# A head's eight output transposes: two at a time between the splits, or all in a row

## The chip, the cores and the metric

The kernel runs on one core of one Trainium2 chip. The metric is the device time of one execution in microseconds; the lower, the better.

## The reference

A decoder trunk of two layers on one sequence of 256 tokens and 2048 channels, in float32. Layer 0 mixes tokens by multi-scale retention with 8 heads (keys of 256, values of 512), layer 1 by a short gated convolution; each layer ends with a SwiGLU of width 5632. What matters here is the end of the retention:

```python
o = rms_norm(chunked_gated_linear_attention(q, k, v, log_a))   # per head: 256 tokens x 512
o = merge_heads(o).astype(h.dtype)
return ((jax.nn.silu(g) * o) @ w_out).astype(h.dtype)
```

For each head, the output is normed per token, multiplied by its gate, and the 8 heads side by side (256 tokens x 4096) are multiplied by `w_out`. All inputs and the result are float32.

## The kernel before

**Numbers in two parts.** Matrix products run in a reduced form of float32 (`F32R`). Each number is therefore kept as a `hi` part (a cast) and a `lo` part (the number less its `hi`), and a product is three partial products: hi by hi, hi by lo, lo by hi. Weights come from memory in pieces of 128 x 2048 (`raw`, three buffers); `prepare` makes of each half a `hi` (ScalarE, L312) and a `lo` (VectorE, L315), 128 x 1024, in a ring of four buffers each. `take` hands TensorE the next 128 columns and keeps two halves prepared ahead (`AHEAD`). The same is done to activations by `split` (L412): a cast on ScalarE (L414) and a subtraction on VectorE (L415), which reads the same source and the result of the cast.

**The layout.** Activations stand turned: channels on the 128 partitions, tokens along the free dimension, so a product gives turned outputs as well. The retention is the exception. `values` gives `v` with tokens on the partitions (`by_token`, L372 to L374), and so does `outputs` (L869) the head's result: two tiles `o` of 128 tokens x 512 channels. Before `w_out` these have to be turned: 2 tiles x 4 blocks of 128 x 128, eight transposes on TensorE (a product with the identity `ident`).

**The order of a head.** `projections` (L915) makes q and k (`packed`, L397 to L399, then `rope`), `values`, `scores`, and the gates `sg`. `mixed` (L856) returns three pieces of work that are put off into the next head: `outputs(0)`, `last_outputs`, `ends`. `ticked` (L340) counts TensorE's steps and runs a piece when `STEPS` = (8, 8, 20) steps have gone by since the one before. So `ends` stands 20 steps behind the outputs, amid the next head's projections; for the fourth and the last head of `HEAD_ORDER` it stands amid the first group of `ret_out`, the product with half of `w_out` (L357, L360). Between `last_outputs` and `ends`, the norm is made: a sum of squares on ScalarE (L872), a root (`roots_of`, L445 on VectorE, L447 on GpSimd), and `o` (L878 on VectorE).

**`ends`.** It goes through the four blocks of 128 channels. Two blocks share a PSUM bank of 128 x 512: block 0 and 1 the first bank, 2 and 3 the second. For each block it turns both `o` tiles into its half of the bank, then splits that half into `mid[n]`, the operand of `ret_out`.

**What sets the order.** TensorE's instructions run in the order of the program text. Those of ScalarE and VectorE are ordered in this stage by a scheduler from a model of their durations. Each engine then works through its list in order and waits on semaphores. There are eight PSUM banks, one tag, given out by `bank()` (L335). The framework puts waits between engines that use one bank, also where they use different halves of it. The modulation vectors are made on the side through the whole kernel: `modulation` (L241) fetches a row block and reduces it on VectorE (L246).

Of the kernel before, what the change touches and what calls it, by code (L numbers as in the profile page):

```python
# [17 lines left out]
P = 128  # L18
# [169 lines left out]
def trunk(ctx: ExitStack, tc: tile.TileContext, x_in, c_in, pos_in, w_mod, cols_in, tab_in, w_all, out):  # L188
    nc = tc.nc
# [7 lines left out]
    def name(s):  # L197
        serial[0] += 1
        return f"{s}_{serial[0]}"

    def tmp(tag, shape=(P, S), dtype=F32, pool=work, bufs=None):
        return pool.tile(list(shape), dtype, tag=tag, name=name(tag), bufs=bufs)
# [24 lines left out]
    inv_freq, ident = tab[:, 0:1], tab[:, 1 : 1 + P]  # L227
# [107 lines left out]
    def bank():  # L335
        return ps.tile([P, 2, S], F32, tag="bank", name=name("bank"))
# [75 lines left out]
    def split(dst, src, at=slice(0, S)):  # L412

        nc.scalar.copy(dst[:, 0, at], src)  # L414
        nc.vector.tensor_tensor(dst[:, 1, at], src, dst[:, 0, at].bitcast(F32), op=ALU.subtract)  # L415
# [12 lines left out]
    def norm_sums(accs):  # L428

        pt = bank()  # L430
        for t in range(2):
            for i, acc in enumerate(accs):
                nc.tensor.matmul(
                    pt[:, 0, t : t + 1], acc[:, t * P : (t + 1) * P], ones[:, 0:1],
                    start=i == 0, stop=i == len(accs) - 1,
                )
        return pt
# [4 lines left out]
    def roots_of(total, n):  # L442

        r = tmp("rs", (P, 2), bufs=4)
        nc.vector.tensor_scalar(r, total, 1.0 / n, EPS, op0=ALU.mult, op1=ALU.add)  # L445
        r2 = tmp("rs", (P, 2), bufs=4)
        nc.gpsimd.tensor_tensor(r2, r, half, op=ALU.pow)  # L447
        return r2
# [117 lines left out]
    with ExitStack() as inner:  # L566
# [52 lines left out]
        def rm_tile(key, dtype=F32):  # L619
            tag_of[key] = free.pop(0)  # L620
            return rm.tile([P, 2, S], dtype, tag=tag_of[key], name=name("rm"))
# [9 lines left out]
        with tc.tile_pool(name="start", bufs=1) as sp:  # L631
# [59 lines left out]
            with tc.manual_schedule(engines={mybir.EngineType.DVE, mybir.EngineType.Activation}):  # L691
# [16 lines left out]
                for i in range(0, D, 2 * S):  # L708
                    pt = bank().rearrange("p a b -> p (a b)")
# [24 lines left out]
                pt = norm_sums([acc[0][:, 0, :]])  # L734
# [65 lines left out]
        mid = [None] * (4 * HEADS)  # L800
# [55 lines left out]
        def mixed(head, both, v, sg):  # L856

            total = tmp("osum", (P, 2), bufs=2)
            pts, os = [], []

            def outputs(t):

                pt = bank().rearrange("p a b -> p (a b)")
                pts.append(pt)
                n = 0
                for jt in range(t + 1):
                    sp = both[jt][:, :, (t - jt) * P : (t - jt + 1) * P]
                    for i, j in ((0, 0), (0, 1), (1, 0)):
                        nc.tensor.matmul(pt, sp[:, i, :], v[:, jt, j, :], start=n == 0, stop=n == 3 * t + 2)  # L869
                        n += 1  # L870
                sq = rp.tile([P, DV], F32, tag="o", name=name("sq"), bufs=2)
                nc.scalar.activation(sq, pt, AF.Square, accum_out=total[:, t : t + 1])  # L872

            def normed_outputs():
                r = roots_of(total, DV)
                for t, pt in enumerate(pts):
                    o = rp.tile([P, DV], F32, tag="o", name=name("o"), bufs=2)
                    nc.vector.scalar_tensor_tensor(o, pt, r[:, t : t + 1], sg[t], op0=ALU.mult, op1=ALU.mult)  # L878
                    os.append(o)

            def last_outputs():
                outputs(1)
                normed_outputs()

            def ends():
                for i in range(4):
                    if i % 2 == 0:
                        pt = bank()
                    for t, o in enumerate(os):
                        nc.tensor.transpose(  # L890
                            pt[:, i % 2, t * P : (t + 1) * P], o[:, i * P : (i + 1) * P], ident
                        )
                    n = 4 * head + i
                    mid[n] = rm_tile(("mid", n), F32R)
                    split(mid[n], pt[:, i % 2, :])

            return list(zip(STEPS, [lambda: outputs(0), last_outputs, ends]))

# [70 lines left out]
    mid = [mpool.tile([P, 2, S], F32R, tag=f"mid{i}", name=name("mid")) for i in range(KT)]  # L969
# [81 lines left out]
```

## Time and profile before

| | |
|---|---|
| median of three runs | 2684.3 us (2682.71 to 2688.37) |
| the profiled execution | 2684.12 us, its span 2682.3 us |
| mean granted clock of TensorE | 0.992 |
| TensorE busy, share of the span | 98% |
| VectorE, ScalarE busy | 74%, 47% |
| memory read | 682.99 MB, 255 GB/s over the span |

The span goes from the first to the last instruction. An engine's busy time is the union of its instructions. TensorE's matmuls are pipelined: the record of one ends after the next could begin, so intervals between starts tell more than lengths. PE is the matmuls, PEld the weight loads in front of them, DVE is VectorE, ACT ScalarE, POOL GpSimd. A row of the timeline gives start, length, engine, line, operation, what is written and read, a count of instructions merged into the row, and in brackets the idle time before it with the instruction that ended it. A row of the waits gives total, number and longest. A row of the windows gives the stretch, then busy time and count for each engine, the granted clock of TensorE (1.00 is full), the share of the transfers and their GB/s.

### The profile page before, as it was taken

The numbers are of one execution on the slowest core, as the hardware profiler recorded it, in microseconds if no ns is written. First come the engines' busy times: TensorE is split into PE (matmuls) and PEld (weight loads), VectorE is DVE, ScalarE is ACT, GpSimd is POOL, SyncE is SP. The second block draws the span as 40 slices with busy tenths as digits, with TensorE's granted clock in tenths as the row PEclk, the third lists the DMA queues.
The fourth block names the chain that finished last, engine by engine and source line by source line (L and its number), as shares of the span: only waits on it lengthen the run. The fifth ranks groups of instructions, "written<-read, shape, count | busy, mean of one in ns | idle before, by whom it ended". The sixth has DMA issues, their size and how long they took to land.

```text
span 2682.3 us, 38239 instructions
## 1 busy us (share of the span) xinstructions
PE 2627.3 (98%) x15220; PEld 2303.8 (86%) x15220; DVE 1993.6 (74%) x2543; ACT 1248.4 (47%) x1770; POOL 145.8 (5%) x230
## 2 busy tenths in 40 slices
PE   7999899999999999999999999999999999999998
PEld 6988789878889888888888898888998888888887
DVE  7997768777678887777777879888886765555564
ACT  5644443444446454334444454444554443444443
POOL 0000000100000001100000001100000000000000
PEclk9999999999999999999999999999999999999999
DMA  9966558866767887777777768776767665555553
GB/s 398 388 269 242 222 192 313 295 226 253 250 223 254 301 307 282 272 279 282 282 273 276 276 221 313 297 281 247 280 252 266 256 230 188 189 189 189 189 189 126
DMA packets 96950, 687.58 MB, mean 256 GB/s; under 512 B 10753, under 2 KB 12545, under 8 KB 13825
## 3 DMA queue, kind: packets, MB, share of 16 engines
q1 hardware_dynamic: 96770, 685.13, 68.8%
q8 instruction: 119, 1.95, 0.3%
q14 instruction: 61, 0.50, 0.0%
HBM read 682.99 MB, written 2.10 MB: 255 GB/s over the span
## 4 chain that ended last, share of the span: by engine, by line
PE 73%; issue 19%; DVE 4%; DMA 2%; ACT 1%; POOL 0%; DVEq 0%; ACTq 0%; POOLq 0%
PE bank L357 34%; PE bank L360 17%; PE bank L372 4%; PE bank L373 4%; PE bank L374 4%; PE bank L399 2%; PE bank L397 2%; PE bank L398 2%; PE bank L517 1%; PE bank L516 1%; PE bank L518 1%; DVE lo L315 1%; DMA raw<-w_all 1%; DVE raw L642 1%; DMA raw<-w_mod 1%
## 5 line engine op out<-in xcount | busy, mean ns | idle before, releaser
L315 DVE TENSOR_TENSOR lo<-raw,hi 128x1024 fp32r<-128x1024 f32 x912 | 1113.5, 1224 | 583.2 <-ACT hi L312 581.1
L312 ACT CAST hi<-raw 128x1024 fp32r<-128x1024 f32 x912 | 955.1, 1052 | 1118.4 <-PE bank L357 644.3
L357 PE MATMUL bank<-h,hi 128*128 128x512 f32 x3296 | 1155.3, 395 | 0.0
L360 PE MATMUL bank<-h,lo 128*128 128x256 f32 x3296 | 924.4, 280 | 0.0
L357 PEld LDWEIGHTS bank<-h,hi 128*128 128x128 f32 x3296 | 622.5, 189 | 145.3
L360 PEld LDWEIGHTS bank<-h,lo 128*128 128x128 f32 x3296 | 622.0, 189 | 0.0
L357 PE MATMUL bank<-mid,hi 128*128 128x512 f32 x1604 | 556.3, 393 | 0.0
L360 PE MATMUL bank<-mid,lo 128*128 128x256 f32 x1604 | 444.9, 277 | 0.1
L246 DVE SCALAR_TENSOR_TENSOR raw<-raw,cb 128x2048 f32<-128x2048 f32 x160 | 365.8, 2286 | 13.7 <-DMA raw<-w_mod 13.5
L357 PEld LDWEIGHTS bank<-mid,hi 128*128 128x128 f32 x1604 | 300.7, 187 | 69.4
L360 PEld LDWEIGHTS bank<-mid,lo 128*128 128x128 f32 x1604 | 301.3, 188 | 0.5 <-DVE lo L315 0.5
L372 PE MATMUL bank<-hi,h 128*128 128x512 f32 x512 | 206.1, 403 | 0.0
L373 PE MATMUL bank<-lo,h 128*128 128x512 f32 x512 | 205.3, 401 | 0.0
L374 PE MATMUL bank<-hi,h 128*128 128x512 f32 x512 | 205.0, 400 | 0.0
L357 PE MATMUL bank<-rm,hi 128*128 128x512 f32 x496 | 177.2, 401 | 0.0
L399 PE MATMUL bank<-h,lo 128*128 128x256 f32 x512 | 147.1, 287 | 6.8 <-DVE lo L315 6.8
L397 PE MATMUL bank<-h,hi 128*128 128x256 f32 x512 | 146.9, 287 | 2.5 <-ACT h L670 2.5
L398 PE MATMUL bank<-h,hi 128*128 128x256 f32 x512 | 146.5, 286 | 0.5 <-DVE h L671 0.5
L360 PE MATMUL bank<-rm,lo 128*128 128x256 f32 x496 | 139.9, 282 | 0.0
L374 PEld LDWEIGHTS bank<-hi,h 128*128 128x128 f32 x512 | 98.4, 192 | 23.4
L372 PEld LDWEIGHTS bank<-hi,h 128*128 128x128 f32 x512 | 98.7, 193 | 20.2
L373 PEld LDWEIGHTS bank<-lo,h 128*128 128x128 f32 x512 | 98.3, 192 | 20.1
(152 smaller groups left out, 2255.3 us busy)
## 6 DMA issues: line engine op xcount, KB each, us to landing
raw<-w_all SPq DMA_DIRECT2D x456, 1024.0 KB, 4.9
raw<-w_mod SPq DMA_DIRECT2D x192, 1024.0 KB, 5.0
x<-x_in SPq DMA_DIRECT2D x4, 512.0 KB, 5.6
out<-out SPq DMA_DIRECT2D x5, 256.0 KB, 2.9
decay<-tab_in SPq DMA_DIRECT2D x8, 128.0 KB, 2.1
out<-out SPq DMA_DIRECT2D x3, 128.0 KB, 2.3
out<-out SPq DMA_DIRECT2D x1, 384.0 KB, 2.7
cols<-cols_in SPq DMA_DIRECT2D x1, 160.0 KB, 8.7
```

The lines of the kernel that those rows point to most:

```text
L246: nc.vector.scalar_tensor_tensor(raw, raw, 1.0, cb, op0=ALU.mult, op1=ALU.mult, accum_out=total)
L312: nc.scalar.copy(hi, raw)
L315: nc.vector.tensor_tensor(lo, raw, hi.bitcast(F32), op=ALU.subtract)
L357: nc.tensor.matmul(pt, hi, h, start=fresh and k == g.ks[0], stop=False, skip_group_check=True)
L360: nc.tensor.matmul(pt[:, 1, :], lo, h[:, 0, :], start=False, stop=last and k == g.ks[-1], skip_group_check=True)
L372: nc.tensor.matmul(o, ht[:, 0, :], hi, start=first, stop=False)
L373: nc.tensor.matmul(o, ht[:, 0, :], lo, start=False, stop=False)
L374: nc.tensor.matmul(o, ht[:, 1, :], hi, start=False, stop=last)
L397: nc.tensor.matmul(pt, hi, h[:, 0, :], start=first, stop=False, skip_group_check=True)
L398: nc.tensor.matmul(pt, hi, h[:, 1, :], start=False, stop=False, skip_group_check=True)
L399: nc.tensor.matmul(pt, lo, h[:, 0, :], start=False, stop=last, skip_group_check=True)
L516: nc.tensor.matmul(pt, hi, rows[0], start=k == 0, stop=False)
```

## The change

The eight transposes are given first, tile by tile instead of block by block, into two banks that are taken at the start; the four splits follow.

```diff
             def ends():
+                turned = [bank() for _ in range(2)]
+                for t, o in enumerate(os):
+                    for i in range(4):
+                        nc.tensor.transpose(
+                            turned[i // 2][:, i % 2, t * P : (t + 1) * P], o[:, i * P : (i + 1) * P], ident
+                        )
                 for i in range(4):
-                    if i % 2 == 0:
-                        pt = bank()
-                    for t, o in enumerate(os):
-                        nc.tensor.transpose(
-                            pt[:, i % 2, t * P : (t + 1) * P], o[:, i * P : (i + 1) * P], ident
-                        )
                     n = 4 * head + i
                     mid[n] = rm_tile(("mid", n), F32R)
-                    split(mid[n], pt[:, i % 2, :])
+                    split(mid[n], turned[i // 2][:, i % 2, :])
```

Everything else is the same. In the built program the scheduler puts a head's four splits into the order of blocks 0, 2, 1, 3, with some pieces of other work between them, where before it was 0, 1, 2, 3. The transposes stand at L889 of the changed kernel (L890 before).

## The prediction

> **What bounds the kernel now.** I read the page first: the busy times, then the chain that ended last.
>
> ```profile
> span 2682.3 us, 38239 instructions
> PE 2627.3 (98%) x15220; PEld 2303.8 (86%) x15220; DVE 1993.6 (74%) x2543; ACT 1248.4 (47%) x1770; POOL 145.8 (5%) x230
> PE 73%; issue 19%; DVE 4%; DMA 2%; ACT 1%; POOL 0%; DVEq 0%; ACTq 0%; POOLq 0%
> ```
>
> TensorE (PE) is busy for 98% of the span and holds 73% of the chain. So a microsecond in which PE stands still is a microsecond of the result, if nothing else is late in its place. The change touches only the eight calls of `ends`, one per head, between 230 and 753 us. The next view is therefore the waits of PE and of its weight loads (PEld) from 225 to 780 us; the two answers have one row each (total us, times, longest).
>
> ```profile
> PE bank L890 <- DVE rm L415: 26.3, 16, 2.5
> PEld bank L890 <- DVE rm L415: 30.0, 16, 2.7
> ```
>
> In that half millisecond PE waits for nothing except this: a transpose (L890) waits for the second half of the split before it (L415 on VectorE), 16 times, twice per head. No row says that PE waits for a `lo` piece, a bank or a transfer. The timeline of the first head (start, length, engine, line, the idle before in brackets) shows why.
>
> ```profile
> 230.27 0.38 PE L890 MATMUL bank<-tab,o 128*128 128x128 f32 x2
> 230.28 1.22 DVE L315 TENSOR_TENSOR lo<-raw,hi 128x1024 fp32r<-128x1024 f32 x1
> 230.93 0.37 ACT L414 CAST rm<-bank 128x256 fp32r<-128x256 f32 x1
> ...
> 232.02 0.42 DVE L415 TENSOR_TENSOR rm<-bank,rm 128x256 fp32r<-128x256 f32 x1
> 232.50 0.42 PEld L890 LDWEIGHTS bank<-tab,o 128*128 128x128 f32 x4 [2.08 <-DVE rm L415]
> 232.50 0.66 PE L890 MATMUL bank<-tab,o 128*128 128x128 f32 x4 [1.85 <-DVE rm L415]
> ...
> 234.29 0.29 PEld L890 LDWEIGHTS bank<-tab,o 128*128 128x128 f32 x2 [1.38 <-DVE rm L415]
> ...
> 234.64 0.78 PE L372 MATMUL bank<-hi,h 128*128 128x512 f32 x1
> ```
>
> Two transposes go into the left half of a bank, ScalarE and VectorE split it, and only then do the next two go into the right half of the same bank. VectorE is still busy with a `lo` piece (230.28) and what stands behind it, so its part comes late, at 232.02. Note the run of four in 0.66 us: it is the right half of the first bank and the left half of the second, and it crosses from bank to bank without a wait. Only the return to a bank that is being read costs.
>
> The stall has a second price. I asked for busy time in stretches of 3.4 us (PE, PEld, DVE, ACT, POOL, then the granted clock), first a pair from the start of the span, which has no transposes, then two that hold stalls:
>
> ```profile
> 152.10:155.50 3.40, 1.48 (x12) 1.45 (x12) 3.40 (x6) 3.18 (x5) 0.00 (x0) 1.00 0.10 39
> 155.50:158.90 3.40, 3.40 (x12) 2.85 (x12) 3.40 (x4) 1.04 (x2) 0.00 (x0) 0.50 0.94 386
> 271.60:275.00 3.40, 1.78 (x10) 1.23 (x8) 3.40 (x4) 1.43 (x2) 0.19 (x1) 1.00 0.76 251
> 377.40:380.80 3.40, 1.59 (x10) 1.26 (x11) 1.53 (x5) 1.02 (x3) 0.00 (x0) 1.00 0.58 178
> ```
>
> then the stretches behind the stalls, of which the first, the last and the sum of all eight:
>
> ```profile
> 234.04:237.45 3.41, 3.15 (x9) 2.57 (x10) 0.63 (x2) 0.37 (x1) 0.00 (x0) 0.50 0.82 271
> ...
> 752.86:756.27 3.41, 3.41 (x13) 2.82 (x12) 1.68 (x2) 0.10 (x1) 0.00 (x0) 0.50 0.40 166
> sum 27.28, PE 26.16 PEld 22.55 DVE 15.47 ACT 4.77 POOL 0.69; mean PE 3.27 PEld 2.82 DVE 1.93 ACT 0.60 POOL 0.09
> ```
>
> After each of the eight stalls the granted clock is 0.50 for 3.41 us. A stretch in which PE was busy 1.59 us or less is followed by such a drop, also without a transpose (152.10 and 155.50); the one with 1.78 us (271.60) is not. What half the clock costs is seen from starts of neighbouring matmuls, wide ones around the second head:
>
> ```profile
> 272.54 0.39 PE L373 MATMUL bank<-lo,h 128*128 128x512 f32 x1
> 272.77 0.39 PE L374 MATMUL bank<-hi,h 128*128 128x512 f32 x1
> ...
> 280.38 0.63 PE L373 MATMUL bank<-lo,h 128*128 128x512 f32 x1
> 280.81 0.63 PE L374 MATMUL bank<-hi,h 128*128 128x512 f32 x1
> ```
>
> and narrow ones around the seventh:
>
> ```profile
> 667.44 0.28 PE L398 MATMUL bank<-h,hi 128*128 128x256 f32 x1
> 667.56 0.28 PE L399 MATMUL bank<-h,lo 128*128 128x256 f32 x1
> ...
> 672.93 0.41 PE L399 MATMUL bank<-h,lo 128*128 128x256 f32 x1
> 673.14 0.41 PE L397 MATMUL bank<-h,hi 128*128 128x256 f32 x1
> ```
>
> Wide ones go from 0.23 to 0.43 us apart, narrow ones from 0.12 to 0.21: 46% and 43% of the time at half clock is lost.
>
> **The change, part by part.** No instruction is added or dropped: 64 transposes, 32 casts and 32 subtractions stay. In the built program the eight transposes of a head stand in a row, four of `o` 0 (two into each bank) and four of `o` 1. What they still wait for is `o` and the earlier owners of the banks.
>
> *The stall.* Weight loads stand idle 30.0 us before L890, matmuls 26.3 us; the second is smaller because a matmul's record ends later than the point at which the next could start. Starts tell which is nearer: in the first head the transposes begin at 230.27 and the next matmul at 234.64, 4.37 us. Two in a row took 0.38 us and four 0.66, so two more cost 0.28 and eight end after 0.66 + 4 x 0.14 = 1.2 us; the next matmul starts before the last record ends (the narrow ones above are 0.28 long and start 0.12 apart), so eight take some 1.0 us of PE. That leaves 3.4 us, and the two idle times of the weight loads there are 2.08 + 1.38 = 3.46. I take 29.5 us for the eight heads, close to PEld's row.
>
> *The clock.* With the eight in a row, the stretch that holds them has at least 3.4 - 1.0 = 2.4 us of other matmuls, above the 1.78 after which no drop came. So I take away all eight drops. In them PE was busy 26.16 us. In four heads the last transposes lie in the drop and are counted above (about 0.3 us each, as 234.29 to 234.64), which leaves 25 us; at 45% lost, 11.3 us.
>
> The Trainium skill speaks against this term in two places of "TensorE: Matmul & The Clock Gate". Its section "Part 4: PE-mode transpose" says that a transpose does not count as PE-busy in the same way; by the 2.4 us above it would not matter here. Its Part 1 (What's actually happening) lets the clock fall after an idle window of some 3.4 us; the trace differs, since the stretch from 377.40 was half busy and a drop followed. By that page alone the drops would not come from these stalls, and might stay: that is a rival below.
>
> *The waits that remain.* The first transposes need `o` (L878), and the second bank is now wanted at once.
>
> ```profile
> 227.02 1.41 DVE L878 SCALAR_TENSOR_TENSOR o<-bank,rs,sg 128x512 f32<-128x512 f32 x2 [0.59 <-POOL rs L447]
> ```
>
> Both `o` end at 228.43, 1.8 us before the first transpose; the chain to them starts at the same head's outputs, whose distance from `ends` is set by a count of PE's own steps, so it doesn't shrink with the stall. The second bank was wanted without a wait before, at 232.50, and its former owner has been done since earlier work. I cost both at nothing; with the cover gone each would be a wait of a microsecond or two per head.
>
> *The splits.* They now lie entirely beside PE's matmuls. A bank's two splits still take turns (cast, subtraction, cast, subtraction), and the queues of ScalarE and VectorE hold weight pieces behind them. The question is whether `hi` and `lo` become late. Pieces go through a ring of four, and ScalarE is the one that waits for PE to let go of one:
>
> ```profile
> ACT hi L312 <- PE bank L374: 105.5, 61, 3.8
> ```
>
> A piece of 1024 columns feeds PE for 12 wide matmuls, 12 x 0.23 = 2.8 us; a freed place is needed again three pieces later, 8.3 us, and filling it takes about a cast of 1.05 and a subtraction of 1.22 us: some 6 us to spare, an estimate. A head's VectorE work in `ends` is 4 x 0.42 = 1.7 us and is not new, but 5 us of PE's pause (stall and drop) go, in which it was done. The tightest place is the second head, where a modulation, a rope and the splits follow one another on VectorE:
>
> ```profile
> 270.11 2.35 DVE L315 TENSOR_TENSOR lo<-raw,hi 128x1024 fp32r<-128x1024 f32 x2
> 272.39 2.28 DVE L246 SCALAR_TENSOR_TENSOR raw<-raw,cb 128x2048 f32<-128x2048 f32 x1
> ...
> 278.85 1.22 DVE L315 TENSOR_TENSOR lo<-raw,hi 128x1024 fp32r<-128x1024 f32 x1
> ```
>
> That `lo` ends at 280.07 now, and in the new order a split more stands ahead of it: 280.5. PE resumes at 273.0 + 1.0 = 274.0; it then has the half piece that it was in, and the two that VectorE finished by 272.4 (270.11, x2): 6 + 12 + 12 = 30 wide matmuls of 0.23, 7 us, so it needs the next at 281. Half a microsecond is left, so I add nothing, and keep a microsecond or two per head for a rival.
>
> **The sum.** 29.5 + 11.3 = 40.8 us. The profiled execution took 2684.12 us (its span is 2682.3), so 2643.3; the runs' median is 2684.3, practically the same. Forecast 2643, 1.5% less. Bounds: with 30.0 and 12.2 (26.16 at 46%) 2642; with 26.3 and 10.8 (25 at 43%) 2647.
>
> **The rivals.** First, **the clock drops stay** though the stall goes (the page's rules, or a gate that sees something else). For it: a drop at 155.50 has nothing to do with transposes. Against it: that one also follows a half idle stretch, and all eight follow stalls. Time: 2684.1 - 29.5 = 2655. Second, **pieces come late** behind the splits: PE waits for `lo` at the second head and its like, 1 to 2 us in each head, 8 to 16 us in all with an occasional drop; 2651 to 2659. For it speaks the half microsecond above; against it that six of the eight heads have more room, and that PE waited for no `lo` in 225 to 780. Third, on the other side, **the queues lock**: ScalarE's cast of a bank's second half waits for VectorE's subtraction of the first, which sits behind other work, and the `hi` casts behind it wait too. It begins to cost when ScalarE is held over the 6 us of the ring, and turns the sign when each head loses more than 40.8 / 8 = 5.1 us. Held 11 us, a head would stand 5 us and pay a drop of 1.5: 8 x 6.5 = 52 us, 2695. Against it: the first split of the first head took from 230.93 to 232.44 (232.02 + 0.42) with a `lo` piece in its way; four such in series are 6 us, not 11. Fourth, **the change does not do it**: the wait is for something other than the bank and PE stops in the same places, 2684. Against it: the run of four crosses banks freely, and both stops stand at a return to a bank.
>
> **How the numbers follow.** Forecast (2639 to 2649) 0.83; drops stay 0.05; pieces late 0.08; no effect 0.02; locked queues 0.02. From no change a measurement of this kernel can tell about 0.2% (5 us): the three runs of before lie 5.7 us apart. Faster 0.96, same 0.02, slower 0.02. The range goes from 2638 (the bound of 2642 less the spread of runs) to 2655, which takes in the drops that stay and half of the late pieces.
>
> **What would show it.** The waits of PE and PEld in the same stretch should have no row for the transposes; each head's eight should take about 1 us to the next matmul; the clock should have none of its drops left behind the heads. `lo` waits of PE in a head mean the second rival. A clock of 0.50 behind transposes that run in a row means the first. If `o` becomes the releaser of the first transpose, the 1.8 us of cover were wrong.

## The result, and the profile after

The changed kernel takes 2643.88 us (median of 5 runs, 2641.89 to 2645.05) beside 2683.73 us for the kernel before (5 runs): a ratio of 0.9851, 95% interval 0.9836 to 0.9865. The forecast was 2643 us, in a range of 2638 to 2655. The profiled execution of the changed kernel took 2641.89 us, its span 2640.1 us.

On the page, the share of PE rises by a hundredth, and in the chain the 4% of VectorE become 2%:

```profile
span 2640.1 us, 38225 instructions
PE 2608.1 (99%) x15220; PEld 2291.2 (87%) x15220; DVE 1990.3 (75%) x2543; ACT 1244.8 (47%) x1770; POOL 146.6 (6%) x230
PE 76%; issue 19%; DVE 2%; DMA 1%; ACT 1%; POOL 0%; DVEq 0%; POOLq 0%; ACTq 0%
```

The waits of PE and PEld from 225 to 745 us, where before each had its one row of 26.3 and 30.0 us, are now empty. The first head's transposes, on PE alone (start, length, line):

```profile
228.52 0.39 PE L374 MATMUL bank<-hi,h 128*128 128x512 f32 x1
228.75 1.03 PE L889 MATMUL bank<-tab,o 128*128 128x128 f32 x8
229.54 0.48 PE L372 MATMUL bank<-hi,h 128*128 128x512 f32 x1
229.86 0.39 PE L373 MATMUL bank<-lo,h 128*128 128x512 f32 x1
230.10 0.39 PE L374 MATMUL bank<-hi,h 128*128 128x512 f32 x1
```

One row of eight stands where three rows with gaps stood, and the next matmul starts 0.79 us after the first transpose, not 4.37. The matmuls behind it start 0.23 us apart, not 0.43. The same stretch of the transposes in all eight heads has PE busy throughout at full clock (the first, the last and the sum of eight windows):

```profile
226.60:230.00 3.40, 3.40 (x21) 2.89 (x20) 3.40 (x8) 2.07 (x4) 0.00 (x0) 1.00 0.50 212
...
707.90:711.30 3.40, 3.40 (x24) 3.08 (x23) 1.47 (x2) 1.62 (x4) 0.00 (x0) 1.00 0.73 289
sum 27.20, PE 27.20 PEld 24.84 DVE 22.24 ACT 14.04 POOL 0.00; mean PE 3.40 PEld 3.10 DVE 2.78 ACT 1.75 POOL 0.00
```

**Where the time went.** From the first transpose to the next matmul, the eight heads take 36.6 us in the trace of before (4.4, 5.5, 4.8, 4.7, 4.7, 3.9, 4.0, 4.7) and 6.3 us in that of after (0.79 or 0.80 each): 30.3 us. From there to the next head's transposes, each of the first seven stretches is 1.2 to 1.6 us shorter with the same matmuls in it (9.8 us), and behind the eighth head the next hundred matmuls take 1.5 us less: 11.4 us for the eight clock drops. Two more differences lie where the programs are the same. Ahead of the first transposes, the execution of before took 1.5 us longer: its clock fell at 42.9 and 155.5 us, and in the other execution it didn't. Far behind the last head, the execution of after took 0.9 us longer, half of it in one wait of TensorE for a `lo` piece at 1824.7 us and half at the very end. These two aren't the change, and they are why the medians, 39.9 us apart, say more than the spans, 42.2 apart.

### The profile page after: what moved, and what is told of

It reads as the page before. It is cut to its first block, busy times and chain, and to the rows that moved or that the text cites. A ratio compares the mean times of both kernels' runs of the same rounds, so it can differ in the third digit from the quotient of the medians.

```text
span 2640.1 us, 38225 instructions
## 1 busy us (share of the span) xinstructions
PE 2608.1 (99%) x15220; PEld 2291.2 (87%) x15220; DVE 1990.3 (75%) x2543; ACT 1244.8 (47%) x1770; POOL 146.6 (6%) x230
## 4 chain that ended last, share of the span: by engine, by line
PE 76%; issue 19%; DVE 2%; DMA 1%; ACT 1%; POOL 0%; DVEq 0%; POOLq 0%; ACTq 0%
PE bank L357 35%; PE bank L360 18%; PE bank L372 4%; PE bank L373 4%; PE bank L374 4%; PE bank L399 2%; PE bank L398 2%; PE bank L397 2%; PE bank L517 1%; PE bank L516 1%; PE bank L518 1%; DVE raw L642 1%; DMA raw<-w_all 1%; PE bank L869 1%; DVE lo L315 1%
## 5 line engine op out<-in xcount | busy, mean ns | idle before, releaser
L357 PE MATMUL bank<-h,hi 128*128 128x512 f32 x3296 | 1155.2, 395 | 0.0
L357 PEld LDWEIGHTS bank<-h,hi 128*128 128x128 f32 x3296 | 622.6, 189 | 145.3
L357 PE MATMUL bank<-mid,hi 128*128 128x512 f32 x1604 | 556.3, 393 | 0.0
L246 DVE SCALAR_TENSOR_TENSOR raw<-raw,cb 128x2048 f32<-128x2048 f32 x160 | 365.4, 2284 | 11.7 <-DMA raw<-w_mod 11.3
L357 PEld LDWEIGHTS bank<-mid,hi 128*128 128x128 f32 x1604 | 300.7, 187 | 69.4
L372 PE MATMUL bank<-hi,h 128*128 128x512 f32 x512 | 202.7, 396 | 0.0
L374 PE MATMUL bank<-hi,h 128*128 128x512 f32 x512 | 201.9, 394 | 0.0
L357 PE MATMUL bank<-rm,hi 128*128 128x512 f32 x496 | 174.2, 396 | 0.0
```

The lines of the kernel that those rows point to most:

```text
L246: nc.vector.scalar_tensor_tensor(raw, raw, 1.0, cb, op0=ALU.mult, op1=ALU.mult, accum_out=total)
L357: nc.tensor.matmul(pt, hi, h, start=fresh and k == g.ks[0], stop=False, skip_group_check=True)
L372: nc.tensor.matmul(o, ht[:, 0, :], hi, start=first, stop=False)
L374: nc.tensor.matmul(o, ht[:, 1, :], hi, start=False, stop=last)
```

## The experiments

The theory: a transpose that goes back to a bank has to wait until the split of the other half is done, and PE, standing still, gets half its clock for the next 3.4 us. The rivals: that the row of eight or its order by tile is what helps; that the clock falls for another reason, such as the transposes themselves; that VectorE has no room behind the splits.

### A bank for each block, in the old order

```diff
             def ends():
+                own = head not in (HEAD_ORDER[3], HEAD_ORDER[7])
                 for i in range(4):
-                    if i % 2 == 0:
+                    if own or i % 2 == 0:
                         pt = bank()
```

> The order of before (two transposes, split, two transposes, split), but in six of the eight heads each of the four blocks has a bank of its own, so that TensorE never returns to a bank that is being read. The fourth and the last head keep the two banks of before. Theory (the stall is the return to a bank whose other half is being split; the clock drop follows from the stall): in the six heads the transposes run in a row with no wait and no drop although the splits stand between them in the program; the two old heads keep 2 x (3.9 stall + 1.4 clock) = 10.6 us, so 2644 + 10.6 = 2654.5 us (2651 to 2658). Rival (what helps is giving all eight ahead of the splits, or the order by tile): the six heads keep their waits, 2675 to 2684 us.

Measured: 2654.38 us (ratio to before 0.9887, 0.987 to 0.9903). The program still gives two transposes, a split, two transposes; in the six heads they run in a row of eight on PE, since no wait stands between them. First the first head, then the fourth, which keeps two banks:

```profile
230.35 1.03 PE L891 MATMUL bank<-tab,o 128*128 128x128 f32 x8
230.79 1.18 ACT L414 CAST rm<-bank 128x256 fp32r<-128x256 f32 x4
231.12 0.19 PEld L372 LDWEIGHTS bank<-hi,h 128*128 128x128 f32 x1
231.15 0.48 PE L372 MATMUL bank<-hi,h 128*128 128x512 f32 x1
```

```profile
358.92 0.38 PE L891 MATMUL bank<-tab,o 128*128 128x128 f32 x2
361.69 0.66 PE L891 MATMUL bank<-tab,o 128*128 128x128 f32 x4 [2.39 <-DVE rm L415]
363.38 0.69 PE L891 MATMUL bank<-tab,o 128*128 128x128 f32 x2 [1.03 <-DVE rm L415]
363.72 0.77 PE L357 MATMUL bank<-rm,hi 128*128 128x512 f32 x1
```

The waits of PE in the stage are those of two heads:

```profile
PE bank L891 <- DVE rm L415: 6.8, 4, 2.4
PEld bank L891 <- DVE rm L415: 7.8, 4, 2.6
```

The two old heads take 4.80 us each to the next matmul, and the clock drops at 362.8 and 721.2 us and behind no other head: with the forecast's 1.4 us for a drop, 2 x (4.80 - 0.79) + 2 x 1.4 = 10.8 us, measured 10.5. So it is the return to the bank, not the order in the program. Note also ScalarE's row: with four banks its casts run four in a row.

### One return left

Blocks 0 and 1 are transposed together and split, then 2 and 3 as before. The edit is against the kernel before; three dots stand for the lines of the transposes and of the splits, which are the same but for their place.

```diff
-                for i in range(4):
-                    if i % 2 == 0:
+                for blocks in ((0, 1), (2,), (3,)):
+                    if blocks[0] % 2 == 0:
                         pt = bank()
...
+                    for i in blocks:
...
+                    for i in blocks:
```

> Blocks 0 and 1 are transposed together and then split; blocks 2 and 3 as before, so one return to a bank is left in each head instead of two. Theory: one wait per head, 1.5 to 4 us long because the split of block 2 now queues behind those of 0 and 1; the clock drop comes only in heads in which a stretch of 3.4 us has PE busy for 1.6 us or less, so in some of the eight. Stall 12 to 25 us and drops 3 to 11 us: 2659 to 2680 us. Rival (the drop follows any stop of PE at this place): eight drops. Rival (the wait is not of the bank): two waits per head and 2684 us, or none and 2644 us.

Measured: 2676.1 us (0.9966, 0.9953 to 0.9979). Half of the returns are gone, but not half of the time:

```profile
PE bank L891 <- DVE rm L415: 23.2, 8, 5.5
```

Eight waits are left, and they are longer, up to 5.5 us where at most 4 was expected. The split that is waited for now stands behind two others and what VectorE has between them: in the second head, the five rope steps from 271.73 to 273.66 us. The first head and the second show when the clock falls. Windows of 3.41 us, each the one that holds the wait and the one behind it:

```profile
229.70:233.11 3.41, 1.92 (x13) 1.51 (x12) 3.41 (x6) 1.80 (x5) 0.00 (x0) 1.00 0.03 7
233.11:236.52 3.41, 3.41 (x16) 2.75 (x15) 1.77 (x3) 1.05 (x1) 0.00 (x0) 1.00 0.71 216
270.66:274.07 3.41, 0.00 (x0) 0.00 (x0) 3.41 (x11) 0.66 (x2) 0.19 (x1) 1.00 0.91 363
274.07:277.49 3.42, 3.02 (x8) 2.46 (x9) 2.51 (x5) 0.71 (x2) 0.00 (x0) 0.50 0.22 91
```

A stop of 1.5 us left PE busy for 1.92 of 3.41 us, and no drop came; the second head's stop took the whole window, and the drop came. There are seven drops behind the eight stops; that of the fifth head, behind the longest wait, lasts two such windows. Not every stop is followed by one, so the rival with eight drops falls, and with eight waits and 2676 us the other falls too.

### Bank by bank

Four transposes into one bank, its two splits, then the same with a bank taken only then. The edit is against the kernel before, cut in the same way.

```diff
-                for i in range(4):
-                    if i % 2 == 0:
-                        pt = bank()
...
+                for blocks in ((0, 1), (2, 3)):
+                    pt = bank()
+                    for i in blocks:
+                        for t, o in enumerate(os):
...
+                    for i in blocks:
```

> Four transposes into the first bank (block by block, both tiles), the two splits of that bank, four transposes into a second bank taken only then, its two splits. Theory: TensorE goes through its own list without a stop, since no transpose returns to a bank behind a split; the eight stand in a row on it and the time is that of the change, 2644 us within 3 us. Rival (both banks up front and the order by tile matter, for instance because the first four then need only one o): one wait per head comes back, 2652 to 2664 us.

Measured: 2643.27 us (0.9846, 0.9832 to 0.9861), no different from the change. Each head takes 0.79 or 0.80 us. One wait for a `lo` piece is in the trace, 0.7 us of a weight load at 459 us, far from any transposes (357 and 514 us). Taking both banks ahead and going by tile do nothing of their own; what counts is that both halves of a bank are written before either is read.

### Each transpose six times

```diff
-                for t, o in enumerate(os):
+                for t, o in [(t, o) for _ in range(6) for t, o in enumerate(os)]:
```

> The changed kernel with the eight transposes of a head issued six times over, 48 in a row, the later ones writing the same values over the earlier; the splits follow. 40 more per head at 0.109 us are 4.4 us, 34.9 us in all. A whole stretch of 3.4 us then holds nothing but transposes, with no stop. Theory (transposes that run in a row keep the clock up as matmuls do; the drop comes from PE standing still): no drop, 2644 + 35 = 2679 us (2675 to 2683). Rival (the page's rule that transposes do not count as PE-busy): after each head the clock falls to 0.50 for 3.4 us, 8 x 1.4 = 11 us more, and more where it falls within the row: 2690 us or above.

Measured: 2677.97 us (0.9976, 0.9966 to 0.9986), 34.1 us above the change. The first and the second head in windows, each the 48 transposes and the 3.4 us behind them:

```profile
229.00:234.20 5.20, 5.20 (x50) 5.20 (x48) 2.17 (x3) 0.43 (x1) 0.00 (x0) 1.00 0.36 102
234.20:237.60 3.40, 3.40 (x17) 2.78 (x16) 2.40 (x4) 2.40 (x5) 0.00 (x0) 1.00 0.38 159
271.20:276.40 5.20, 5.20 (x50) 5.19 (x48) 4.51 (x9) 0.88 (x2) 0.00 (x0) 1.00 0.32 129
276.40:279.80 3.40, 3.40 (x18) 2.79 (x16) 2.38 (x6) 2.40 (x5) 0.00 (x0) 1.00 0.33 140
```

The clock stays at 1.00 through 5.2 us that hold almost nothing but transposes, and behind them, in all eight heads. The price is that of the steps: 5.16 us in place of 0.79 per head, 35.0 us. The rival falls: for these float32 transposes, a row of them keeps the clock up. The Trainium skill's "TensorE: Matmul & The Clock Gate", section "Part 4: PE-mode transpose", says that the full clock doesn't engage for the transpose mode; these 5.2 us at 1.00 differ, and the measurement decides here. The trace calls the transposes MATMUL and doesn't show whether they use the mode that the page means. PE waits for `lo` and `hi` pieces in three places between 454 and 480 us, up to 1.2 us, again far from any transposes.

### More work for VectorE

Six additions of 128 x 224 are put between the transposes and the splits; they read the second bank and write to a tile (`scratch`, its declaration not shown) that nobody reads.

```diff
+                for _ in range(6):
+                    nc.vector.tensor_tensor(scratch, turned[1][:, 1, :224], cb[:, :224], op=ALU.add)
```

> The changed kernel with six extra VectorE additions of 128 x 224 per head, each about 0.38 us, placed between the transposes and the splits and writing to a scratch tile that nobody reads: 2.3 us of VectorE per head, 18 us in all. It measures how much room the weight pieces have behind the splits. Theory (some 6 us to spare in most heads, half a microsecond in the second): PE waits for a lo piece in the second head only, about 1 us, and for none in the others; 2644 to 2647 us. Rival (VectorE is at its limit in these stretches): each head loses most of the 2.3 us, 2655 to 2664 us, with lo rows among PE's waits in every head.

Measured: 2646.13 us (0.9861, 0.9845 to 0.9878), 2.3 us above the change for 48 x 0.385 = 18.5 us of VectorE. The waits of PE and PEld from 225 to 760 us:

```profile
PE bank L357 <- DVE rm L415: 1.7, 2, 0.9
PEld bank L357 <- DVE rm L415: 2.8, 4, 1.2
PEld bank L373 <- DVE lo L315: 0.2, 1, 0.2
```

The size is as expected and the place is not. The second head's `lo` made the weight load wait for 0.2 us, not 1. The rest is in the fourth and the last head, where `ret_out` (L357) waits for a `mid` of the very head, 10 to 12 us behind the first transpose: there the splits have a reader soon, which the working of the prediction had left out. The rival (2.3 us in every head) falls.

### The splits first, the returns kept

The kernel before, with one line more:

```diff
-                    split(mid[n], pt[:, i % 2, :])
+                    with tc.high_priority(offset=2000):
+                        split(mid[n], pt[:, i % 2, :])
```

> The kernel before with one thing added: the casts and subtractions of the splits are given a high priority with the scheduler, so that they stand ahead of weight pieces and rope steps in the lists of ScalarE and VectorE. The transposes and the returns to a bank stay as before. It tells how much of a stall is the hand-over itself (a cast of 0.37 and a subtraction of 0.42 us, with the signals between engines some 1.1 us) and how much is the queue in front of it. Theory (both returns stay, only the queue goes): still 16 waits, 1.1 to 1.5 us each, 18 to 24 us in place of 30, with the clock drops left in most heads: 2672 to 2679 us; the change needs to take the return away to get the rest. Rival (the queue is all of it): the waits go and the time falls to 2644 to 2652 us. Rival (the priority moves nothing that counts): 2684 us.

Measured: 2678.51 us (0.9978, 0.9968 to 0.9988).

```profile
PE bank L890 <- DVE rm L415: 23.6, 16, 2.4
PEld bank L890 <- DVE rm L415: 27.4, 16, 2.7
```

All 16 waits stay. The time lies within what was expected, the waits do not: 27.4 us of weight loads standing idle, where 18 to 24 was written down. The first head tells why: the priority moved nothing there, the split still comes behind the `lo` piece and the rope step.

```profile
230.34 1.22 DVE L315 TENSOR_TENSOR lo<-raw,hi 128x1024 fp32r<-128x1024 f32 x1
...
231.47 0.68 DVE L814 TENSOR_TENSOR k<-qa,k 128x512 fp32r<-128x512 f32 x1
232.08 0.41 DVE L415 TENSOR_TENSOR rm<-bank,rm 128x256 fp32r<-128x256 f32 x1
...
232.54 0.42 PEld L890 LDWEIGHTS bank<-tab,o 128*128 128x128 f32 x4 [1.91 <-DVE rm L415]
```

Where the queue was short (the sixth and the seventh head, 1.2 and 1.4 us from the last transpose ahead of a return to the first behind it), the hand-over itself is left. So the reordering can take at most 30 - 16 x 1.2 = 11 us of the wait, an estimate; it took 2.6. The time fell by more, 5.9 us beside the kernel before in the same series (2684.44): in the profile the third and the sixth head have no drop, where in the trace of before all eight have one.

## Why the prediction was right, step by step

- **PE sets the end** (right). 39.9 us were saved where 40.8 were worked out, and no wait of PE is left in the stage. That the forecast lies within 1 us of the median is luck, since the runs of the changed kernel alone lie 3 us apart; that the terms came out is not.
- **The stall, 29.5 us** (right). 30.3 by the starts. The row of PEld (30.0) was the one to take and the row of PE (26.3) the wrong one, as the prediction argued from starts. The transposes start 0.11 us apart and eight take 0.79, where 1.0 was used: 1.7 us in eight heads, which is more than the 0.8 us by which the term was short.
- **The clock, 11.3 us** (right). 11.4 us, and no drop behind any of the heads. The two old heads of the first experiment brought back two drops, the 48 transposes none, so stop and drop belong together. The boundary was put between 1.59 and 1.78 us of PE busy in 3.4 us. It can't be drawn so from the records: in the profile after, a stretch near the start was followed by no drop at 1.58:

```profile
150.58:153.99 3.41, 1.58 (x8) 1.12 (x6) 3.41 (x5) 1.64 (x4) 0.00 (x0) 1.00 0.02 7
153.99:157.40 3.41, 3.32 (x22) 3.06 (x23) 3.41 (x6) 2.10 (x3) 0.00 (x0) 1.00 0.62 231
```

  The records of PE end later than its work. Each matmul can be counted instead from its start for the usual time to the next one (0.23 us for a wide one, 0.12 for a narrow one, 0.11 for a transpose, twice that at half clock), an estimate. The drops of an execution begin whole multiples of 3.413 us apart (in the trace of before the last head's drop comes 208 of these steps after 42.89 us), so its stretches lie on a grid. Counted like this on the grids of all eight traces, up to the last 20 to 60 us of each, the 31 stretches that a drop followed hold at most 1.37 us of work, and none of the others at full clock holds less than 1.38. The stretch from 377.40, with a drop, holds 1.23, and the one from 150.58, without, 1.42. So the two no longer contradict each other; how wide the margin really is, the estimate can't say.

  One thing the term took for granted: that the eight drops of one execution stand for all. A stop that two stretches of the grid share may have none, as in two heads of the last experiment. The 13 runs of before beside the first four experiments took from 2678.21 us, at a mean granted clock of 0.995, to 2690.64 at 0.989; the profiled execution, at 0.992, was a usual one.
- **The waits that remain, at nothing** (right). `o` ends 2.0 us ahead of the first transpose in the first head, and the second bank is had at once.
- **The weight pieces, at nothing** (right, and as near as was said). In the second head of the profile after, VectorE's list and the first use:

```profile
268.21 0.68 DVE L911 TENSOR_TENSOR qs<-rm,bank 128x512 f32<-128x512 f32 x1
...
272.80 3.48 DVE L315 TENSOR_TENSOR lo<-raw,hi 128x1024 fp32r<-128x1024 f32 x3
```

```profile
274.68 0.39 PE L373 MATMUL bank<-lo,h 128*128 128x512 f32 x1
```

  The first of the three pieces ends some 1.2 us after 272.80, at 274.0, and PE takes it at 274.68: 0.7 us of room, where half a microsecond was worked out from the trace of before. In the stretches right behind the other heads' transposes it is over 3 us, less than the 6 us that were estimated, and enough.
- **The rivals.** That the drops stay would have given 2655; that pieces come late, 2651 to 2659; neither is there. The locked queues would have shown ScalarE's casts waiting for VectorE's subtraction in the same bank, and the `hi` casts behind them. Both are there, but short, at most 1.3 and 1.0 us where the rival needed more than 6:

```profile
ACT rm L414 <- DVE rm L415: 4.6, 4, 1.3
ACT hi L312 <- ACT rm L414: 1.8, 3, 1.0
```

What stays open: the early drops at 42.9 and 155.5 us, which come in some executions and not in others. By the records, the stretches ahead of them held 1.15 and 1.48 us; in the profile after, where the grid lies otherwise, the stretches nearest to these places held 1.87 and 1.58, and no drop came. That the grid alone decides it was not tested.

## What to carry to other kernels

Before a bank is shared by two results, ask in which order it is written and read. If the second half is written after the first has been handed to a reader, the writer waits for that reader and its whole queue; writing both halves first, or a bank for each, cost nothing here, and three different orders of program text gave it alike. When TensorE is the bound, look behind each stop of a microsecond or two for a lower granted clock: here it added a third to the price of the stop. Whether a stop is followed by a drop differs between executions, so look at more than one.

## What the runs showed of the hardware

- Transposes of 128 x 128 in float32 start 0.11 us apart (from the first to the next matmul eight take 0.79 us, 48 take 5.16), though each record is 0.27 us long, and they hold the clock at 1.00.
- The clock fell by half for 3.41 us after a stretch of that length in which PE had, by the estimate from starts, at most 1.37 us of work, and at 1.38 and above it didn't; a whole idle stretch was not needed. With a wide matmul each 0.43 us in place of 0.23, a drop was worth 1.2 to 1.6 us.
- Halving the number of waits took their total only from 26.3 to 23.2 us, because the ones that were left were for a split behind a longer queue (the longest 5.5 us, where 2.5 was the longest before).
